# An inverse transform as three passes on high and low parts, in a Hyena and mLSTM encoder layer

## The chip, the cores and the metric

The kernel runs on one core of a Trainium2 chip. The metric is the device time of one execution in microseconds, as the median of several. A core has TensorE (PE in the profile: matrix products into PSUM banks), VectorE (DVE), ScalarE (ACT), GpSimd (POOL) and SyncE (SP), which here only issues DMAs. Each engine runs its own instructions in the order in which they stand in its queue, and waits at an instruction until the others have delivered what it needs.

## The reference

One encoder layer on 2048 rows of 1024 features: a projection, a Hyena group (512 channels) beside an mLSTM group, an output projection, cross-attention to 256 memory rows, and a feed-forward part. What the change touches is the Hyena group's long convolution, made twice (order 0 and order 1) with a filter as long as the sequence, in the frequency domain with zero padding to 4096:

```python
def _hyena(hy, spec, skip):
    L = hy.shape[1]
    u = hy.astype(jnp.float32)
    z, g1, g2 = u[..., :D_HYENA], u[..., D_HYENA:2 * D_HYENA], u[..., 2 * D_HYENA:]
    for o, gate in enumerate((g1, g2)):
        conv = jnp.fft.irfft(jnp.fft.rfft(z, n=2 * L, axis=1) * spec[:, o], n=2 * L, axis=1)[:, :L]
        z = gate * (conv + z * skip[o].astype(jnp.float32))
    return z
```

All data are float32.

## The kernel before, in words

The transform of length 4096 is split into two smaller ones, each done as matrix products on TensorE. In `hyena` (from L789) the first, `spectrum` (L879), multiplies the signal with the matrix `f1` and stores the result in DRAM (`zs0`, `zs1`). The second runs in a loop over 16 blocks (L903), each of two matrices `m`. For each matrix:

- L915 multiplies the loaded signal `t` with the forward matrix `dm[:, m]` into a PSUM bank `pp`; this is a full-precision float32 product, as all those of `hyena` are.
- `response` (L838) has done the same with the filter's block one block ahead; its results are `hr` and `hi`.
- L917 and L918 (ACT) write the bank's two halves, swapped and with a sign, to `xt`; L919 (DVE) multiplies the bank with `hr` into `y`; L920 (POOL) multiplies `xt` with `hi`; L921 (DVE) adds both into `y`. That is the product of two complex spectra.
- `back` (L871) multiplies `y` with the inverse matrix `em[:, m]` (L873) into a bank `pg`; L874 (ACT) copies the bank to `gs`, and after the second matrix L877 (ACT's queue) stores `gs` to DRAM (`zg0`, `zg1`).

`late` (L865) holds `back` of one matrix until the next matrix has been issued, so that the program writes the inverse product one step after its `y`. `load2` (L830) loads, one block ahead, a block's two inverse matrices `em` (128 KB, SP's queue, two buffers) and the signal's block from `zs` (L835). `load_filter` (L821) loads the forward matrices and the filter's block. `xt` and `y` share five buffers (`tb`, tile name `b`); the large tiles (`ta`, name `a`) share ten. After the 16 blocks, a loop over 8 (L926) loads `zg`, multiplies with `e2` and applies the gate; in order 0 that result is the input of order 1.

All this is woven with the input projection (`sweep`, L644, and `natural`, L758): its generator and `hyena`'s are called in turns by the weights that they yield. The projection, like most of the kernel, already computes in three passes. `split` (L341) makes from a float32 tile a high part (`CAST` on ACT, into the type float32r) and a low part (a subtraction on DVE); `mm3` (L336) then issues three matmuls into one bank, high by high, high by low and low by high, on L338, L339 and L340. So these helper lines stand in the profile for every such product, and the tile names tell them apart: `wh`, `wl` are the projection's weights, `xh`, `xl` its input, `mm` its banks, `hy` the banks of `hyena`.

The program's own order is not the order on the engines: a list scheduler, which orders the instructions by a timeline of its own, sets each engine's queue when the kernel is built. A change in one place can thus move instructions near it, on every engine.

Of the kernel before, what the change touches and what calls it, by code (L numbers as in the profile page):

```python
# [9 lines left out]
F32 = mybir.dt.float32  # L10
F32R = mybir.dt.float32r
# [9 lines left out]
CH = 512  # L21
# [111 lines left out]
class Prog:  # L133
# [655 lines left out]
    def hyena(self, es):  # L789
        nc, tc, a = self.nc, self.tc, self.a  # L790
# [7 lines left out]
        def of_block(d, k):  # L798
            return d[4 * k:4 * k + 8].rearrange("(k r) j c -> (r j) k c", k=2)

        sb = es.enter_context(tc.tile_pool(name="h_sb", bufs=1, side="right"))

        def ta():
            return sb.tile([128, 2, CH], F32, tag="a", name="a", bufs=10)

        def tb():
            return sb.tile([128, CH], F32, tag="b", name="b", bufs=5)

        f1 = sb.tile([128, 128], F32, name="f1")
        e2 = sb.tile([128, 64], F32, name="e2")  # L810
        nc.sync.dma_start(out=f1, in_=a["c_f1"])
# [2 lines left out]
        def load1(j2):  # L814
            z = ta()
            js = slice(2 * j2, 2 * j2 + 2)
            for g in range(2):
                nc.sync.dma_start(out=z[own[g]], in_=hy[0, g, :, js])
            return z

        def load_filter(o, i):  # L821
            dm = sb.tile([128, 2, 128], F32, tag="dm", name="dm", bufs=3)
            nc.sync.dma_start(out=dm, in_=a["c_dm"][:, 2 * i:2 * i + 2])
            p, k = divmod(2 * i, 16)
            t = ta()
            for g in range(2):
                nc.sync.dma_start(out=t[own[g]], in_=of_block(fs[o][p, 64 * (p ^ g):64 * (p ^ g) + 64], k))
            return dm, t

        def load2(o, i):  # L830
            em = sb.tile([128, 2, 128], F32, tag="em", name="em", bufs=2)
            nc.sync.dma_start(out=em, in_=a["c_em"][:, 2 * i:2 * i + 2])
            t = ta()
            for g in range(2):
                nc.sync.dma_start(out=t[own[g]], in_=of_block(sds[o][g], 2 * i))  # L835
            return em, t
# [28 lines left out]
        def late(f):  # L865
            if held:
                held.pop()()
            if f is not None:
                held.append(f)

        def back(m, i, em, y, gs, dst):  # L871
            pg = self.hy()
            nc.tensor.matmul(pg, em[:, m], y, start=True, stop=True)  # L873
            nc.scalar.copy(gs[:, m], pg)  # L874
            if m == 1:
                for g in range(2):
                    nc.scalar.dma_start(out=of_block(dst[g], 2 * i), in_=gs[own[g]])  # L877
# [11 lines left out]
        q, fq = [load1(0), load1(1)], []  # L889
# [8 lines left out]
        for o in range(2):  # L898
            gd = gds[o]
            nxt = load2(o, 0)  # L900
            ready = response(0, *fq.pop(0))
            yield 4
            for i in range(16):  # L903
                yield 4.6
                dm, hr, hi = ready
                em, t = nxt
                if i < 14:
                    fq.append(load_filter(o, i + 2))
                if i < 15:
                    nxt = load2(o, i + 1)  # L910
                    ready = response(i + 1, *fq.pop(0))
                gs = ta()
                for m in range(2):
                    pp = self.hy()
                    nc.tensor.matmul(pp, dm[:, m], t[:, m], start=True, stop=True)  # L915
                    xt, y = tb(), tb()
                    nc.scalar.activation(xt[0:64], pp[64:128], AF.Copy, scale=-1.0)  # L917
                    nc.scalar.copy(xt[64:128], pp[0:64])  # L918
                    nc.vector.tensor_tensor(y, pp, hr[:, m], ALU.mult)  # L919
                    nc.gpsimd.tensor_tensor(xt, xt, hi[:, m], ALU.mult)  # L920
                    nc.vector.tensor_tensor(y, y, xt, ALU.add)  # L921
                    late(lambda m=m, i=i, em=em, y=y, gs=gs: back(m, i, em, y, gs, gd))
            late(None)
            nxt = load3(o, 0)
            yield 5
            for j2 in range(8):  # L926
# [14 lines left out]
                y = gate.rearrange("q j (g e) -> q (j g) e", g=8)  # L941
# [542 lines left out]
    def halves(self, src, tags, bufs, eng):  # L1484
        hi, lo = (self.R.tile([128, 512], F32R, tag=n, name=n, bufs=bufs) for n in tags)
        self.nc.scalar.copy(hi, src)  # L1486
        eng.tensor_tensor(lo, src, hi.bitcast(F32), ALU.subtract)  # L1487
        return hi, lo
# [416 lines left out]
```

## Time and profile before

| | us |
|---|---|
| median of 3 timed runs | 3238.39 |
| lowest and highest of them | 3231.79, 3245.16 |
| the profiled execution's own time | 3240.22 |
| its span in the trace | 3238.5 |
| PE busy | 3052.5 |
| DVE busy | 2033.4 |
| ACT busy | 1502.4 |
| POOL busy | 1245.8 |
| mean granted TensorE clock | 0.979 of full |

The span is what the trace shows from the first instruction to the last; the time has a little around it. "Busy" sums the instructions of an engine; matmuls overlap at their ends, so a duration in a PE row is longer than what it adds to PE's stream, which is read from start to start. In the rows, L873 is a line of the kernel, `hy<-b,em` is what it writes and reads, and `x128` a count. A full-precision product is recorded as two matmuls. Where a row says that an instruction waited, the last of its releasers is named.

The inverse products run in two stretches: order 0 from 415 to 602 us and order 1 from 762 to 950 us of the span.

### The profile page before, as it was taken

The page shows a single profiled execution, that of the slowest core. Times are in us where ns is not written, and L with a number is a line of the kernel's source. Part 1 is how long each engine was busy: PE and PEld are TensorE (multiplying, and loading weights), DVE is VectorE, ACT ScalarE, POOL GpSimd, SP SyncE. Part 2 cuts the span into 40 slices and gives each one's busy share as a digit, 9 for nine tenths or more (in the row PEclk, how much of TensorE's full clock was granted, in tenths as well). Part 3 has the DMA queues.
Part 4 walks back from the last instruction along what each step waited for, and adds up shares of the span by engine and source line. Part 5 has one row for each costly group of instructions (what it writes and reads, how often), then busy time and mean ns, then how long its engine had stood idle before and what let it go on. Part 6 is the DMA issues. An engine that isn't in the chain of part 4 may idle for free.

```text
span 3238.5 us, 45244 instructions
## 1 busy us (share of the span) xinstructions
PE 3052.5 (94%) x15241; PEld 2438.0 (75%) x15241; DVE 2033.4 (63%) x3414; ACT 1502.4 (46%) x2873; POOL 1245.8 (38%) x863
## 2 busy tenths in 40 slices
PE   7999899999999876999999998999999999999998
PEld 5655466776668775898988897888788887888876
DVE  7775366447657644776665556656755676566695
ACT  5533366426752423454453445555555543333335
POOL 0122022101213125435251207776855483434483
PEclk9999999999999988999999999999999999999999
DMA  5564768777778598667484537665644475444434
GB/s 187 190 206 162 263 183 221 214 246 199 207 203 262 171 295 261 189 203 230 130 289 131 190 100 233 212 207 165 215 150 153 160 240 160 137 134 149 124 94 166
DMA packets 451634, 617.72 MB, mean 191 GB/s; under 512 B 39615, under 2 KB 247615, under 8 KB 450377
## 3 DMA queue, kind: packets, MB, share of 16 engines
q1 hardware_dynamic: 415268, 556.31, 55.7%
q10 hardware_dynamic: 36132, 58.51, 5.4%
q8 instruction: 121, 1.98, 0.3%
q14 instruction: 113, 0.92, 0.1%
HBM read 416.47 MB, written 198.21 MB: 190 GB/s over the span
## 4 chain that ended last, share of the span: by engine, by line
PE 48%; DMA 9%; DVE 4%; issue 3%; POOL 2%; ACT 2%; SPq 0%; ACTq 0%; DVEq 0%; POOLq 0%
PE mm L340 10%; PE mm L338 10%; PE mm L339 10%; PE hy L340 5%; PE hy L338 5%; PE hy L339 5%; DVE wl L343 1%; DMA wn<-in_xa_wv_dram 1%; DMA va<-vd 1%; DMA wr<-xs 1%; DMA wn<-in_w_out_dram 1%; DMA vw<-o 1%; DMA hg<-hg 1%; ACT wh L343 1%; PE hy L1173 1%
## 5 line engine op out<-in xcount | busy, mean ns | idle before, releaser
L343 DVE TENSOR_TENSOR wl<-wn,wh 128x512 fp32r<-128x512 f32 (+1 forms) x364 | 286.3, 820 | 136.2 <-ACT wh L343 135.7
L1487 DVE TENSOR_TENSOR bl<-wr,bh 128x512 fp32r<-128x512 f32 x213 | 241.7, 1141 | 124.6 <-ACT bh L1486 122.8
L1486 ACT CAST ah<-w 128x512 fp32r<-128x512 f32 x284 | 176.2, 622 | 299.7 <-PE hy L339 154.3
L343 ACT CAST wh<-wn 128x512 fp32r<-128x512 f32 (+1 forms) x364 | 208.7, 617 | 214.6 <-PE mm L339 51.6
L920 POOL TENSOR_TENSOR b<-b,a 128x512 f32<-128x512 f32 x64 | 88.7, 1387 | 519.7 <-ACT b L918 492.4
L338 PE MATMUL mm<-xh,wh 128*128 128x512 f32 x640 | 278.3, 436 | 4.6 <-ACT xh L498 2.3
L339 PE MATMUL mm<-xl,wh 128*128 128x512 f32 x640 | 262.1, 410 | 3.9 <-DVE xl L343 3.4
L1487 DVE TENSOR_TENSOR al<-w,ah 128x512 fp32r<-128x512 f32 x236 | 223.6, 949 | 56.9 <-ACT ah L1486 56.5
L340 PE MATMUL mm<-xh,wl 128*128 128x512 f32 x640 | 256.4, 401 | 0.0
L1486 ACT CAST bh<-wr 128x512 fp32r<-128x512 f32 x232 | 143.6, 620 | 233.8 <-PE mm L340 178.6
L340 PE MATMUL mm<-bh,al 128*128 128x512 f32 x576 | 225.3, 394 | 7.9 <-DVE al L1487 5.1
L338 PE MATMUL mm<-bh,ah 128*128 128x512 f32 x576 | 226.6, 393 | 0.2
L339 PE MATMUL mm<-bl,ah 128*128 128x512 f32 x576 | 225.6, 392 | 0.0
L338 PE MATMUL mm<-act,wh 128*128 128x512 f32 x512 | 200.6, 396 | 1.9 <-ACT wh L343 1.9
L339 PE MATMUL mm<-act,wh 128*128 128x512 f32 x512 | 201.5, 394 | 0.0
L340 PE MATMUL mm<-act,wl 128*128 128x512 f32 x512 | 199.8, 393 | 0.0
L1343 POOL TENSOR_TENSOR ssum<-ssum,sq 128x512 f32<-128x512 f32 x56 | 80.8, 1443 | 277.9 <-ACT sq L1342 274.7
L338 PE MATMUL hy<-bh,ah 128*128 128x512 f32 x448 | 175.2, 391 | 0.0
L339 PE MATMUL hy<-bl,ah 128*128 128x512 f32 x448 | 174.6, 390 | 0.0
L340 PE MATMUL hy<-bh,al 128*128 128x512 f32 x448 | 174.4, 390 | 0.0
L338 PEld LDWEIGHTS mm<-xh,wh 128*128 128x128 f32 x640 | 121.5, 190 | 64.6 <-issue 27.4
L339 PEld LDWEIGHTS mm<-xl,wh 128*128 128x128 f32 x640 | 121.5, 190 | 60.0 <-issue 29.1
(369 smaller groups left out, 8825.8 us busy)
## 6 DMA issues: line engine op xcount, KB each, us to landing
wr<-hc SPq DMA_DIRECT2D x224, 256.0 KB
w<-in_ff_w_dram SPq DMA_DIRECT2D x176, 256.0 KB
hc<-t SPq DMA_DIRECT2D x128, 256.0 KB
wn<-in_w_in_dram SPq DMA_DIRECT2D x100, 256.0 KB
hc<-q SPq DMA_DIRECT2D x96, 256.0 KB
fs<-a SPq DMA_DIRECT2D x32, 512.0 KB
a<-fs SPq DMA_DIRECT2D x64, 256.0 KB
a<-zs SPq DMA_DIRECT2D x64, 256.0 KB
```

What stands on the lines that cost most here:

```text
L338: mm(ps, lh, rh, start=start, stop=False)
L339: mm(ps, lh, rl, start=False, stop=False)
L340: mm(ps, ll, rh, start=False, stop=stop)
L343: both = (self.nc.scalar.copy(hi, src), self.nc.vector.tensor_tensor(lo, src, hi.bitcast(F32), ALU.subtract))
L920: nc.gpsimd.tensor_tensor(xt, xt, hi[:, m], ALU.mult)
L1173: nc.tensor.matmul(dst, nm[:, h], va[:, h], start=True, stop=state is None)
L1343: nc.gpsimd.tensor_tensor(ssum, ssum, sq, ALU.add)
L1486: self.nc.scalar.copy(hi, src)
L1487: eng.tensor_tensor(lo, src, hi.bitcast(F32), ALU.subtract)
```

## The change

The inverse product L873 becomes three passes. `load2` loads the pair of inverse matrices into one raw buffer (`e`, one in place of two) and splits it into high and low parts, two new buffers of each. When `y` is finished, it is split as well: ACT casts it to `vh`, DVE subtracts to get `vl`, again two buffers of each. `back` gets the parts and calls `mm3`. The helpers `split` and `mm3` are as before. The forward products (L842, L915), `f1` and `e2` stay in full precision.

```diff
+        def halves(n):
+            return [sb.tile([128, n], F32R, tag=f"{q}{n}", name=q, bufs=2) for q in ("vh", "vl")]
+
...
         def load2(o, i):
-            em = sb.tile([128, 2, 128], F32, tag="em", name="em", bufs=2)
-            nc.sync.dma_start(out=em, in_=a["c_em"][:, 2 * i:2 * i + 2])
+            e = sb.tile([128, 2, 128], F32, tag="em", name="em", bufs=1)
+            nc.sync.dma_start(out=e, in_=a["c_em"][:, 2 * i:2 * i + 2])
+            em = [t.rearrange("p (m q) -> p m q", m=2) for t in halves(256)]
+            self.split(*em, e)
             t = ta()
...
-        def back(m, i, em, y, gs, dst):
+        def back(m, i, em, vh, vl, gs, dst):
             pg = self.hy()
-            nc.tensor.matmul(pg, em[:, m], y, start=True, stop=True)
+            self.mm3(pg, em[0][:, m], em[1][:, m], vh, vl, True, True)
             nc.scalar.copy(gs[:, m], pg)
...
                     nc.vector.tensor_tensor(y, y, xt, ALU.add)
-                    late(lambda m=m, i=i, em=em, y=y, gs=gs: back(m, i, em, y, gs, gd))
+                    vh, vl = halves(CH)
+                    self.split(vh, vl, y)
+                    late(lambda m=m, i=i, em=em, vh=vh, vl=vl, gs=gs: back(m, i, em, vh, vl, gs, gd))
```

Over the whole program this takes 64 full-precision products from PE and puts 192 passes in their place; ACT gets 64 casts of 512 columns and 32 of 256, and DVE as many subtractions. POOL's order stays the same. On the other engines the scheduler moves instructions in and around both stretches. (In the changed file the lines behind L808 count 3 to 7 higher: L842 is L847, L874 is L879, L915 is L920, L917 and L918 are L922 and L923.)

PE, some blocks into order 0, before. `mm<-xh,wh` and its kin are the projection's passes, `hy<-b,em` an inverse product, `hy<-a,dm` a forward one.

```order
L340 MATMUL mm<-xh,wl 128x512
L873 MATMUL hy<-b,em 128x512 [waits DMAHW3_49,DVE_49]
L915 MATMUL hy<-a,dm 128x512 [waits DMAHW2_49,DMAHW1_49,Activation_49]
L873 MATMUL hy<-b,em 128x512 [waits DVE_49]
L915 MATMUL hy<-a,dm 128x512 [waits Activation_49]
L338 MATMUL mm<-xh,wh 128x512
L339 MATMUL mm<-xl,wh 128x512
L340 MATMUL mm<-xh,wl 128x512
```

PE, some blocks into order 0, in the changed kernel; `hy<-vh`, `hy<-vl,vh` and `hy<-vh,vl` are the three passes of one inverse product.

```order
L340 MATMUL mm<-xh,wl 128x512
L847 MATMUL mm<-a,dm 128x512 [waits DMAHW2_49,DMAHW5_49,DMAHW1_49,Activation_49]
L338 MATMUL hy<-vh 128x512 [waits Activation_49]
L920 MATMUL hy<-a,dm 128x512 [waits DVE_49]
L847 MATMUL mm<-a,dm 128x512 [waits DVE_49,PE_49]
L339 MATMUL hy<-vl,vh 128x512 [waits DVE_49]
L340 MATMUL hy<-vh,vl 128x512
L338 MATMUL mm<-xh,wh 128x512 [waits Activation_49]
```

The one product is now three rows. The first waits for ACT's cast alone and stands ahead of two other products here; the second waits for DVE's subtraction.

ACT, in the middle of a block of order 0, before: `b<-hy` writes `xt`, `a<-hy` copies the inverse product's bank, `zg` is the store, `wh<-wn` a part of the projection's weights, `P` and `cv` belong to the projection.

```order
L917 ACTIVATE b<-hy 64x512 [waits PE_49]
L918 COPY b<-hy 64x512
L343 CAST wh<-wn 128x512 [waits DMAHW4_49]
L874 COPY a<-hy 128x512 [waits PE_49]
L917 ACTIVATE b<-hy 64x512 [waits PE_49]
L918 COPY b<-hy 64x512
L877 DMA zg_2437<-a 64x2x512 [waits DMAHW1_49,Activation_49]
L877 DMA zg_2437<-a 64x2x512 [waits DMAHW2_49]
L706 ACTIVATE cv<-cv 128x1008 [waits DVE_49]
L687 COPY P<-mm 128x512 [waits PE_49]
```

ACT, in the middle of a block of order 0, in the changed kernel; `vh<-b` is the cast of `y`, `vh<-em` that of the matrices.

```order
L922 ACTIVATE b<-hy 64x512 [waits PE_49]
L923 COPY b<-hy 64x512
L343 CAST vh<-b 128x512 [waits DVE_49]
L343 CAST vh<-em 128x256 [waits DMAHW3_49,PE_49]
L879 COPY a<-hy 128x512 [waits PE_49]
L882 DMA zg_2437<-a 64x2x512 [waits Activation_49]
L882 DMA zg_2437<-a 64x2x512 [waits DMAHW4_49]
L687 COPY P<-mm 128x512 [waits PE_49]
L343 CAST vh<-b 128x512 [waits DVE_49]
L701 ACTIVATE cv<-P,par 128x1008 [waits DMAHW0_49,Activation_49]
```

Two new kinds of rows stand ahead of the bank copies L879 and L687: the cast of `y`, which waits for DVE, and the cast of the matrices, which waits for their load and for a product on PE.

SP, one block's loads in order 0, before: `em` are the inverse matrices, `dm` the forward ones, `fs` the filter's block, `zs` the signal's, `wn` and `qt` belong to the projection.

```order
L832 DMA em<-in_c_em_dram 128x256 [waits DMAHW7_49,PE_49]
L823 DMA dm<-in_c_dm_dram 128x256 [waits DMAHW0_49,PE_49]
L372 DMA wn<-in_w_in_dram 128x2x256 [waits DMAHW4_49,DMAHW3_49,DVE_49]
L733 DMA qt<-cv 128x1008 [waits Activation_49]
L827 DMA a<-fs_347 64x2x512 [waits DMAHW5_49]
L827 DMA a<-fs_347 64x2x512 [waits DMAHW6_49]
L835 DMA a<-zs_2435 64x2x512 [waits DMAHW7_49]
```

SP, one block's loads in order 0, in the changed kernel.

```order
L826 DMA dm<-in_c_dm_dram 128x256 [waits DMAHW1_49,PE_49]
L372 DMA wn<-in_w_in_dram 128x2x256 [waits DMAHW4_49,DMAHW2_49,DVE_49]
L835 DMA em<-in_c_em_dram 128x256 [waits DMAHW3_49,DVE_49]
L830 DMA a<-fs_347 64x2x512 [waits DMAHW6_49]
L830 DMA a<-fs_347 64x2x512 [waits DMAHW7_49]
L840 DMA a<-zs_2435 64x2x512 [waits DMAHW0_49]
```

The load of the inverse matrices has moved behind that of the forward ones, and it waits for DVE (the subtraction that frees the raw buffer) where it waited for PE.

## The prediction

> **What bounds the kernel now.** I read the page first for the share of each engine.
>
> ```profile
> span 3238.5 us, 45244 instructions
> ...
> PE 3052.5 (94%) x15241; PEld 2438.0 (75%) x15241; DVE 2033.4 (63%) x3414; ACT 1502.4 (46%) x2873; POOL 1245.8 (38%) x863
> ```
>
> TensorE is busy for 94% of the span; no other engine comes near. That is a mean over stages, so I then read the busy times in windows over the stretch in which the inverse products run. The columns are the window, its length, then busy time and count of PE, PEld, DVE, ACT and POOL, the granted TensorE clock, the DMA share and GB/s.
>
> ```profile
> core 0: us, PE busy (x) PEld busy (x) DVE busy (x) ACT busy (x) POOL busy (x), PEclk, DMA share, GB/s
> ...
> 400.00:520.00 120.00, 117.91 (x421) 77.77 (x420) 80.02 (x117) 82.36 (x133) 26.91 (x19) 1.00 0.71 193
> 520.00:640.00 120.00, 114.37 (x590) 85.35 (x590) 61.78 (x98) 62.49 (x108) 19.03 (x13) 0.97 0.78 224
> 640.00:760.00 120.00, 116.34 (x664) 84.24 (x662) 59.45 (x89) 44.33 (x77) 2.56 (x2) 0.97 0.73 223
> 760.00:880.00 120.00, 117.17 (x426) 77.11 (x425) 80.12 (x118) 81.21 (x135) 25.39 (x19) 1.00 0.72 202
> 880.00:960.00 80.00, 78.42 (x314) 54.49 (x314) 50.22 (x73) 51.52 (x83) 14.82 (x11) 1.00 0.68 189
> ```
>
> PE is idle for 2.1 + 5.6 + 3.7 + 2.8 + 1.6 = 15.8 of these 560 us, while ACT and DVE are busy for some two thirds of the windows where the spectra are multiplied (82.36 and 80.02 of 120). So in this stage the end is set by TensorE's own stream: PE time saved here moves everything behind it forward, and work added to ACT and DVE costs only where PE comes to wait for it.
>
> A busy PE is not the same as PE time used, because matmuls overlap, so I take costs from start to start in PE's timeline (start, duration, what).
>
> ```profile
> 467.33 1.02 PE L873 MATMUL hy<-b,em 128*128 128x512 f32 x2
> 468.19 1.02 PE L915 MATMUL hy<-a,dm 128*128 128x512 f32 x2
> 469.05 1.02 PE L873 MATMUL hy<-b,em 128*128 128x512 f32 x2
> 469.90 1.02 PE L915 MATMUL hy<-a,dm 128*128 128x512 f32 x2
> ...
> 470.99 0.39 PE L339 MATMUL mm<-xl,wh 128*128 128x512 f32 x1
> ...
> 477.15 0.39 PE L339 MATMUL mm<-xl,wh 128*128 128x512 f32 x1
> ```
>
> A full-precision product, which the trace records as two matmuls, takes (469.90 − 467.33) / 3 = 0.857 us from start to start. The two L339 rows are the first and last of an unbroken run of three-pass products, 27 matmuls apart: 6.16 / 27 = 0.228 us for one pass, 0.684 for three.
>
> **The change part by part.**
>
> *Three passes for one product (removed and added on PE).*
>
> ```profile
> L873 PE MATMUL hy<-b,em x128: 590/592/697, 415.0 to 949.6; 128*128 128x512 f32 x128
> ...
>   DVE b L921: 2.1, 2
> ```
>
> These 128 records are 64 products, two in each of 16 blocks, for both orders. Each gives 0.857 − 0.684 = 0.173 us, together 64 × 0.173 = 11.0 us, on the engine that sets the end. The price of three passes is taken from the same lines 338 to 340 at the same shape, so it is well known; −11.0 is the firm term. The Trainium skill, in "FP8 and Floating Point Precision", section "TensorE Precision Notes", says that a true FP32 product makes four passes. By that rule the saving would be one pass for each product, 64 × 0.228 = 14.6 us, and the sum below −10.4 in place of −6.8; the trace differs, since its product takes 0.857 / 0.228 = 3.8 passes, and the sum goes by the trace.
>
> *The parts (added on ACT and DVE).* The casts and subtractions have neighbours of the same form in the weights' parts, and a 128x256 ACT copy is near the cast of the matrices.
>
> ```profile
> L343 ACT CAST wh<-wn x20: 612/620/652, 409.8 to 582.6; 128x512 fp32r<-128x512 f32 x16, 128x544 fp32r<-128x544 f32 x4
> ```
>
> ```profile
> L343 DVE TENSOR_TENSOR wl<-wn,wh x59: 677/685/1102, 410.9 to 956.4; 128x512 fp32r<-128x512 f32 x51, 128x544 fp32r<-128x544 f32 x8
> ```
>
> ```profile
> L779 ACT COPY st<-mm 128x256 f32<-128x256 f32 x19 | 7.1, 372 | 39.0 <-PE mm L340 19.0 <-DMA vd<-st 6.2 <-DMA wn<-in_w_in_dram 4.8
> ```
>
> A block gets on ACT 2 × 0.620 + 0.372 = 1.6 us, on DVE 2 × 0.685 and one subtraction of 256 columns. Nothing in this stage shows that last one; it lies between half the 512-column row and all of it, 0.34 to 0.69, and I take 0.5, the middle, since these rows hold a fixed part too: 1.9 us. How long is a block? SP loads one pair of inverse matrices for each:
>
> ```profile
> 433.79 0.36 SPq L832 DMA_DIRECT2D em<-in_c_em_dram  x1
> ...
> 470.10 0.33 SPq L832 DMA_DIRECT2D em<-in_c_em_dram  x1
> ```
>
> These are four issues, three blocks: 36.31 / 3 = 12.1 us. Of that ACT is busy 82.36 / 120 × 12.1 = 8.3 us and DVE 80.02 / 120 × 12.1 = 8.1. After the change they stand at 9.9 and 10.0, each with some 2.2 us of a block left. So the added 32 × (1.6 + 1.9) = 112 us lie beside PE's stream, at a price of nothing, as long as that cover of 2.2 us a block holds.
>
> *The longer way to each product (a wait on PE).* Behind y now come the cast and the subtraction, 0.620 + 0.685 = 1.3 us, before the last two passes can start. How early is y today?
>
> ```profile
> L921 DVE TENSOR_TENSOR b<-b x64: 670/691/1769, 409.7 to 944.2; 128x512 f32<-128x512 f32 x64
> ```
>
> I set the end of each L921 in the timeline beside the start of its L873, from the first pair (409.7 and 415.0) to the last (944.2 and 949.6), 64 pairs. y is done 3.0 to 8.0 us ahead in 56 of them, 1.8 ahead in one, 0.1 or less in seven; the median is 4.7. So 57 products have room for the 1.3 us, even though the queues are fuller. The seven would each wait 1.3 more if the order stayed, 9.2 us in all. But the order was made anew with the parts in it, and it sets the first pass, which needs only the cast, ahead of the other two, with other matmuls between in 52 of 64 cases. The nearest row is what the present order leaves PE waiting for y, 2.1 us (above). With two engines in the way in place of one I take twice that, +4.2, between 0 and 9.2.
>
> *The matrices' parts and the queues.* One raw buffer in place of two, and its release moves from PE to DVE. SP now loads the next pair when the subtraction is done, not when the product of the block before last has run:
>
> ```profile
> SPq L832 <- PE hy L873: 85.7, 23, 7.8
> ```
>
> 85.7 us of standing on SP go, with the spectra's loads queued behind. What PE waits for from those loads bounds the gain:
>
> ```profile
>   DMA a<-zs: 3.5, 2
> ```
>
> ```profile
>   DMA a<-fs: 5.0, 2
> ```
>
> That is 0 to 8.5 us. I take 0: the wait has not gone, it has moved. The cast of the matrices' high part now waits on ACT, for the load and for the product that frees its buffer, and the filter's matrices still stand on SP behind a wait for PE. On ACT the cast mostly (20 of 32 times) stands right ahead of a copy that itself waits for an inverse product, so it adds little there. The early release of y's buffer (five are shared by xt and y) can only help and is taken at 0.
>
> *The ends of the loops.* After each order's last product come the copy, the store and the load for the next stage. The last pair has room (above), so 0; without that room it is 1.3 for each order, 2.6 in all.
>
> Sum: −11.0 + 4.2 + 0 + 0 + 0 = −6.8 us. The profiled execution took 3240.2, 1.7 us around its span of 3238.5, and would take 3233.4. The median of the three timed runs, 3238.4, lies 1.8 below it; on it I set 3231.6.
>
> **The rivals.**
>
> *No change.* The wait for the parts gives the 11.0 back: 0.17 us for each product, or eight of the 64 waiting the full 1.3. For it: seven stand at the edge already, and both engines lose near half of their slack. Against: the first pass needs only the cast, and the median room is 4.7. Time 3238.4.
>
> *Slower: ACT stands for y.* ACT takes its instructions in order, and the cast of y waits for POOL's product and DVE's sum. Behind it in ACT's row stand the copies that empty the banks which PE waits for (L687, and the copy of the inverse product). Today nothing on ACT waits for y.
>
> ```profile
> L920 POOL TENSOR_TENSOR b<-b,a x64: 1267/1292/2714, 405.3 to 942.8; 128x512 f32<-128x512 f32 x64
> ```
>
> If each cast of y comes right behind xt, ACT stands 1.29 + 0.69 = 2.0 us for it, 4.0 a block. 2.2 are left, so PE loses 1.8 in each of 32 blocks, 57 us, less 11: +46, 3284. It decides from ACT standing over 2.2 us a block; a loss of 0.5% (16 us) needs (16 + 11) / 32 = 0.8 more, 3.0 a block, three quarters of the worst case. For it: L921's longest of 1769 ns against its median of 691, and POOL's 2714 against 1292, show that DVE and POOL can hold each other up, and 96 more subtractions of that kind meet POOL's 64 products. The Trainium skill, "SBUF — State Buffer", section "Who interferes with whom", has a rule for this, that a VectorE instruction with two SBUF inputs contends with a GpSimd instruction that reads SBUF; the trace agrees in those two longest times. Against: in the new order one to a dozen other instructions stand between xt and that cast, and those fill most of the 2.0 us.
>
> *More than the sum.* The loads come early, the 8.5 us go, and no new wait comes: −11.0 − 8.5 = −19.5, 3218.9. For it: SP's 85.7 us. Against: two short waits for zs hold 3.5 of it, and the order of SP's row changed too.
>
> That the change does not do what it says is hardly open: three passes of this shape run in the same stretch at a price that the trace shows.
>
> **How the numbers follow.** The forecast, −2 to −15, has 0.60; no change 0.18; slower 0.10; more than the sum 0.12. 0.5%, 16 us, is about what a measurement of this kernel can tell from no change (its three runs lie 13.4 apart). The forecast and no change lie within it, but for 0.05 of the forecast whose end, with a part of the loads' gain, reaches over. Faster by over 0.5%: 0.12 + 0.05 = 0.17. Slower: 0.10 less 0.01 for a mild case, 0.09. Same: 0.74. The range goes down to 3218, which takes in the best sum, and up to 3247: there PE loses (8.6 + 11.0) / 32 = 0.6 us a block, the mild part of the slower case. Outside lie the rest of the slower case and the trace's noise, under 2 in 10.
>
> **What would show it.** In the changed profile the triples on hy should start 0.23 us apart when unbroken; the weights' wait L338 to L340 on the parts should sum to about 4 us; ACT and DVE should be busy some 99 of the 120 us between 400 and 520; SP's wait ahead of the em load should be gone, or name DVE and be short; the last inverse product should start some 5 to 10 us earlier than 949. I am wrong if PE's idle time between 400 and 960 is over 27 us (15.8 + 11), or if ACT stands for y over 2 us a block, or if PE's idle time falls below 10 us.

## The result, and the profile after

| | us |
|---|---|
| changed kernel, median of 4 runs | 3262.03 (3259.89 to 3263.27) |
| before, median of 4 runs beside it | 3240.47 (3231.79 to 3245.16) |
| ratio, 95% interval | 1.0069, 1.0046 to 1.0092 |
| span of the profiled execution, before and after | 3238.5, 3261.5 |

The change makes the kernel 0.7% slower, by some 22 us. The forecast was 3231.6, within 3218 to 3247, so both the value and the sign of the difference were wrong.

First the page of the changed kernel, span and busy times:

```profile
span 3261.5 us, 45538 instructions
...
PE 3059.2 (94%) x15305; PEld 2460.3 (75%) x15305; DVE 2088.0 (64%) x3510; ACT 1543.8 (47%) x2969; POOL 1247.6 (38%) x863
```

PE's share is the same 94% and says nothing of the loss. The windows of the stretch with the inverse products do (columns as in the prediction: window, length, busy time and count of PE, PEld, DVE, ACT and POOL, granted clock, DMA share, GB/s):

```profile
400.00:520.00 120.00, 113.00 (x416) 78.79 (x414) 91.12 (x134) 86.41 (x148) 26.82 (x18) 0.97 0.69 184
520.00:640.00 120.00, 109.09 (x547) 85.28 (x548) 80.63 (x128) 76.78 (x138) 22.03 (x14) 0.94 0.71 205
640.00:760.00 120.00, 117.12 (x712) 85.33 (x712) 53.64 (x80) 39.48 (x72) 0.00 (x0) 1.00 0.77 243
760.00:880.00 120.00, 111.90 (x429) 78.27 (x428) 91.92 (x139) 86.28 (x150) 24.69 (x18) 0.99 0.73 192
880.00:960.00 80.00, 73.27 (x274) 50.98 (x273) 60.37 (x93) 60.81 (x104) 15.45 (x12) 0.98 0.64 185
```

PE is idle for 7.0 + 10.9 + 2.9 + 8.1 + 6.7 = 35.6 us, where it was 15.8 before. The prediction had named 27 as the bound beyond which it would be wrong. In the stretch between the loops, 640 to 760, nothing is lost (2.9 against 3.7): the loss lies in the two loops over the 16 blocks. Their length is read from the weight loads of the forward product, one group for each order, from the first to the last start. Before:

```profile
L915 PEld LDWEIGHTS hy<-a,dm x64: 186/190/192, 401.3 to 594.5; 128*128 128x128 f32 x64
```

```profile
L915 PEld LDWEIGHTS hy<-a,dm x64: 186/189/192, 752.4 to 939.1; 128*128 128x128 f32 x64
```

The changed kernel:

```profile
L920 PEld LDWEIGHTS hy<-a,dm x64: 186/189/337, 403.9 to 608.3; 128*128 128x128 f32 x64
```

```profile
L920 PEld LDWEIGHTS hy<-a,dm x64: 186/188/192, 763.8 to 962.1; 128*128 128x128 f32 x64
```

The loop of order 0 grew from 193.2 to 204.4 us, that of order 1 from 186.7 to 198.3: 11.2 + 11.6 = 22.8 us, against 23.0 between the spans. Each loop now holds 5.5 us less of product time (half of the 11.0), and takes 11 us more. Windows over the two loops, the first two before, the last two in the changed kernel:

```profile
401.30:594.50 193.20, 186.28 (x685) 123.76 (x684) 131.11 (x192) 133.35 (x218) 43.35 (x30) 0.98 0.72 199
752.40:939.10 186.70, 182.81 (x662) 120.69 (x661) 125.84 (x185) 127.07 (x209) 40.17 (x30) 1.00 0.71 198
...
403.90:608.30 204.40, 187.19 (x715) 132.77 (x716) 160.08 (x237) 151.39 (x260) 46.27 (x30) 0.95 0.67 187
763.80:962.10 198.30, 184.27 (x700) 128.71 (x701) 149.53 (x230) 147.02 (x254) 40.40 (x31) 0.98 0.68 186
```

PE is idle for 10.8 us of the loops before and for 31.2 after: 20.4 of the 22.8. It is also busy for 2.4 us longer, in spite of the shorter products, at a granted clock of 0.95 and 0.98 where it was 0.98 and 1.00.

What does PE wait for there? These are rows of its waits between 400 and 990 us (waiting tile and line, releaser, us in total, times, longest). Before, the copy of the filter's bank by DVE (L846) has one row:

```profile
PE mm L721 <- DVE a L846: 0.4, 1, 0.4
```

In the changed kernel the same copy is L851:

```profile
PE mm L338 <- DVE a L851: 10.0, 6, 4.4
...
PE mm L721 <- DVE a L851: 2.6, 1, 2.6
PE hy L339 <- DVE vl L343: 2.5, 1, 2.5
...
PE hy L338 <- ACT vh L343: 1.5, 4, 0.5
...
PE mm L727 <- DVE a L851: 1.2, 1, 1.2
...
PE mm L847 <- DVE a L851: 1.1, 1, 1.1
```

All rows of the view sum to 20.5 us before (15 rows) and to 39.4 after (20 rows). For the parts themselves, where the prediction had looked, PE waits 2.5 + 1.5 = 4.0 us. For L851 it waits 10.0 + 2.6 + 1.2 + 1.1 = 14.9: of the 18.9 more, 14.5 are these. Most are waits of the projection's products (`mm`), which have no data from the changed product at all.

One place shows how that comes about. `response` writes the filter's product into one of the four `mm` banks, the same that the projection uses, and ACT (L848, L849) and DVE (L850, L851) copy it out. Here is PE in the changed kernel, some rows between 502 and 522 us:

```profile
502.47 1.02 PE L847 MATMUL mm<-a,dm 128*128 128x512 f32 x2
...
504.61 1.10 PE L847 MATMUL mm<-a,dm 128*128 128x512 f32 x2 [1.11 <-ACT cv L706]
```

```profile
516.68 1.96 PE L847 MATMUL mm<-a,dm 128*128 128x512 f32 x4
521.18 0.47 PE L338 MATMUL mm<-xh,wh 128*128 128x512 f32 x1 [2.54 <-DVE a L851]
```

And DVE at the same place:

```profile
515.66 0.69 DVE L924 TENSOR_TENSOR b<-hy,a 128x512 f32<-128x512 f32 x1 [3.77 <-ACT b L923]
...
517.95 0.69 DVE L924 TENSOR_TENSOR b<-hy,a 128x512 f32<-128x512 f32 x1 [0.18 <-ACT b L923]
518.56 1.04 DVE L343 TENSOR_TENSOR vl<-em,vh 128x256 fp32r<-128x256 f32 x1
519.64 0.69 DVE L850 COPY a<-mm 64x512 f32<-64x512 f32 x1
520.34 0.69 DVE L851 COPY a<-mm 64x512 f32<-64x512 f32 x1
```

And the last of ACT's copies of the same bank:

```profile
518.84 0.58 ACT L849 COPY a<-mm 64x512 f32<-64x512 f32 x1
```

The products of one block's response were made at 502.47 and 504.61 (two records each). The first of their banks is not emptied until 521.03, since DVE's copies stand in its row behind two spectra's products (L924) of the block in progress and a subtraction of the matrices; and DVE itself stood for 3.77 us ahead of 515.66, for ACT's copy of a forward product (L923). ACT's copies come late as well, the last at 518.84; DVE's end last. At 516.68 PE makes the next block's two response products. Now all four `mm` banks hold responses, no pass of the projection can start, and PE stands from 518.64 until 521.18, 0.15 us after L851's end. Before, the same pair of products and its copies at a like place were this:

```profile
499.65 1.88 PE L842 MATMUL mm<-a,dm 128*128 128x512 f32 x4
...
510.32 1.88 PE L842 MATMUL mm<-a,dm 128*128 128x512 f32 x4
```

```profile
506.40 0.69 DVE L846 COPY a<-mm 64x512 f32<-64x512 f32 x1
...
508.44 0.69 DVE L846 COPY a<-mm 64x512 f32<-64x512 f32 x1
```

Both banks are empty at 509.13, before the next pair at 510.32. I set the end of each response product beside the end of its L846 or L851, 64 pairs for each kernel: the median is 6.4 us before and 10.6 after. For ACT's last copy (L844, L849) it is 4.8 and 8.9, so the whole response is emptied later, by both engines, and DVE's copy is the last of the four for all 64. The time to DVE's copy, "time to empty", is used below for every kernel; it is an evaluation of the same rows, not a view of its own.

Standing costs PE more than the stand itself, since the granted clock falls behind it. Two places in the changed kernel, in windows, and the longest stand, which lies at the second of them:

```profile
502.97:506.38 3.41, 1.62 (x4) 0.30 (x2) 3.32 (x6) 3.35 (x6) 0.52 (x1) 1.00 0.80 267
506.38:509.79 3.41, 3.40 (x8) 2.72 (x9) 3.38 (x7) 1.27 (x3) 1.25 (x1) 0.50 0.49 108
...
591.72:595.13 3.41, 1.86 (x9) 0.91 (x7) 3.41 (x7) 3.33 (x6) 2.69 (x2) 1.00 0.47 129
...
598.54:605.37 6.83, 6.00 (x25) 5.93 (x26) 3.83 (x7) 3.15 (x6) 0.00 (x0) 0.50 0.61 189
```

```profile
599.37 0.56 PE L338 MATMUL mm<-wh,xh 128*128 128x272 f32 x1 [4.39 <-DVE a L851]
```

At the first place PE stood for 1.11 us (ahead of 504.61, above) and for 0.69, and then had a clock of 0.50 for 3.41 us, in which passes of 512 columns start 0.43 us apart, where they start 0.23 apart at full clock: about half of that time is lost. At the second the clock is at 0.50 from 595.13, the beginning of the stand of 4.39 us (594.98 to 599.37), to 605.37, so that about half of the 6.00 us in which PE is busy behind the stand, 3 us, is lost on top of it. Around the stand of 2.54 us that ends at 521.18 the clock stayed at 1.00. The Trainium skill, "TensorE: Matmul & The Clock Gate", section "Part 1: The HAM clock gate", says that the clock falls to half after an idle window of about 3.4 us; these rows do not agree with it, since PE was busy for 1.62 and 1.86 of the 3.41 us ahead of the two falls. In the nine falls of both kernels between 400 and 990 us PE had been busy for 22 to 55% of the 3.41 us ahead (worked out from the same traces).

### The profile page after: what moved, and what is told of

Read it like the earlier page. It is cut to its first block, busy times and chain, and to the rows that moved or that the text cites. A ratio compares the mean times of both kernels' runs of the same rounds, so it can differ in the third digit from the quotient of the medians.

```text
span 3261.5 us, 45538 instructions
## 1 busy us (share of the span) xinstructions
PE 3059.2 (94%) x15305; PEld 2460.3 (75%) x15305; DVE 2088.0 (64%) x3510; ACT 1543.8 (47%) x2969; POOL 1247.6 (38%) x863
## 4 chain that ended last, share of the span: by engine, by line
PE 55%; DMA 8%; DVE 5%; issue 3%; ACT 2%; POOL 2%; SPq 0%; ACTq 0%; DVEq 0%; POOLq 0%
PE mm L338 12%; PE mm L340 12%; PE mm L339 12%; PE hy L338 5%; PE hy L340 5%; PE hy L339 5%; DVE bl L1494 1%; DMA rw<-rows 1%; DVE wl L343 1%; DMA wr<-xs 1%; DMA wn<-in_xa_wo_dram 1%; PE hy L1180 1%; ACT wh L343 1%; PE hy L1182 1%; DMA wn<-in_w_out_dram 1%
## 5 line engine op out<-in xcount | busy, mean ns | idle before, releaser
L321 POOL TENSOR_TENSOR b<-b 128x512 f32<-128x512 f32 x32 | 59.1, 1847 | 274.2 <-PE mm L721 120.3
```

The source lines that it names most:

```text
L321: nc.gpsimd.tensor_tensor(e[1], f, b, ALU.subtract)
```

## The experiments

The letters in the expectations are the theories of the time: A, the parts load ACT and DVE; B, the three passes cost more than the product; C, any new order of the queues gives or takes as much; D and E, the parts have too few buffers; F, the first pass, set early, holds its bank; G, the way of a matrix from forward product to copied result (13.5 us before, 17.3 after, medians) is longer, and the program keeps only so many matrices under way; H, the large buffers are held longer. What the section above shows of the response's banks became my theory (R) only when all runs were in. "x" is the ratio to the kernel before, timed beside each. The last two columns are of the one profiled execution, whose own time can lie off the median (by 14 us in e5, 13 in e9); in e13 and e17 the sum of waits holds one of 4.6 and 4.5 us that lies ahead of the window but for its end.

| kernel | median us | x, 95% interval | PE waits 400 to 990 | time to empty, median |
|---|---|---|---|---|
| before | 3240.47 | 1 | 20.5 | 6.4 |
| changed | 3262.03 | 1.0069, 1.0046 to 1.0092 | 39.4 | 10.6 |
| e1_passes_only | 3224.03 | 0.9966, 0.9951 to 0.9981 | 21.5 | 4.9 |
| e2_parts_unused | 3239.70 | 1.0014, 1.0001 to 1.0028 | 24.5 | 6.2 |
| e3_act_only | 3242.60 | 1.0015, 0.9999 to 1.0030 | 22.0 | 5.5 |
| e4_dve_only | 3234.51 | 0.9995, 0.9982 to 1.0008 | 18.8 | 6.5 |
| e5_y3 | 3252.25 | 1.0052, 1.0025 to 1.0079 | 35.2 | 10.6 |
| e6_em3 | 3255.22 | 1.0052, 1.0034 to 1.0070 | 37.1 | 9.9 |
| e7_y_parts | 3257.72 | 1.0059, 1.0039 to 1.0078 | 35.8 | 10.1 |
| e8_em_parts | 3223.22 | 0.9951, 0.9936 to 0.9966 | 18.6 | 5.8 |
| e9_low_first | 3280.31 | 1.0139, 1.0114 to 1.0165 | 55.0 | 14.5 |
| e10_early_hold | 3236.26 | 0.9992, 0.9981 to 1.0002 | 16.8 | 4.5 |
| e11_low_first_pool | 3287.49 | 1.0156, 1.0142 to 1.0170 | 55.6 | 14.2 |
| e12_null | 3239.78 | 1.0004, 0.9993 to 1.0016 | 22.5 | 6.4 |
| e13_late2 | 3232.61 | 0.9974, 0.9962 to 0.9987 | 20.7 | 4.9 |
| e14_filler | 3282.95 | 1.0135, 1.0121 to 1.0149 | 40.3 | 11.1 |
| e15_dve_cast | 3256.44 | 1.0056, 1.0042 to 1.0069 | 33.6 | 9.6 |
| e16_a11 | 3263.41 | 1.0068, 1.0055 to 1.0081 | 36.7 | 10.6 |
| e17_both3 | 3248.94 | 1.0035, 1.0021 to 1.0048 | 36.2 | 9.7 |
| e18_before_late2 | 3217.94 | 0.9942, 0.9927 to 0.9957 | 11.5 | 3.8 |

### Which part of the change costs

**e1_passes_only** issues the three passes but makes no low parts: `y` is rounded by its own addition and stands for both parts, and the matrices are cast once.

```diff
-                    vh, vl = halves(CH)
-                    self.split(vh, vl, y)
+                    vh = vl = y
...
-            self.split(*em, e)
+            nc.scalar.copy(em[0], e)
```

> The inverse product runs as three passes, but y is written rounded and used as both of its parts, and the matrices are only cast once (a cast of 256 columns on ACT in each block), so the output lacks the low parts. No work on DVE is added. Theory A (the parts' work on ACT and DVE delays the copies that free the banks, and PE waits for banks): the saving of the passes shows nearly whole, 3240 - 11 = 3229, with PE's lost time in both stretches as before. Rival B (the passes themselves are the cost: a bank held longer, or the second pass waiting): still 3250 or more. Rival C (the new order by itself, whatever work it holds): anything between 3225 and 3265.

Measured 0.9966: 11 us faster, as the prediction's −11.0 for the passes. B falls.

**e2_parts_unused** makes all parts as the changed kernel does and then multiplies in full precision with the raw tiles (the raw matrices have two buffers, as before the change).

```diff
-            self.mm3(pg, em[0][:, m], em[1][:, m], vh, vl, True, True)
+            nc.tensor.matmul(pg, em[:, m], y, start=True, stop=True)
```

> All parts are made as in the changed kernel, but the inverse product stays one full-precision product of the raw tiles; the parts are read by nobody. Theory A: the loss without the saving, 3262 + 11 = 3273. Rival B: no loss, 3240. Rival C: anything between 3230 and 3265.

**e3_act_only** is e2 with the casts alone, **e4_dve_only** with subtractions alone (a tile minus itself); nothing reads them.

```diff
-                    self.split(vh, vl, y)
+                    nc.scalar.copy(vh, y)                               # e3
+                    nc.vector.tensor_tensor(vh, y, y, ALU.subtract)     # e4
```

> Only ACT's share of the parts is made (the casts of y and of the matrices), read by nobody; the product is the full-precision one. Theory A with DVE as the engine that matters (the banks that PE waits for are freed by a DVE copy): 3240 to 3248. Theory A with ACT as that engine (the cast of y stands in ACT's row for POOL and DVE): 3258 to 3273. Rival B: 3240.

> Only DVE's share is made: a subtraction of 512 columns behind each y and one of 256 for each pair of matrices, with no cast (the tile minus itself), read by nobody; the product is the full-precision one. Theory A with DVE as the engine that matters: 3258 to 3273. With ACT: 3240 to 3248. Rival B: 3240.

Measured 1.0014, 1.0015 and 0.9995. In e2 both engines do all the added work, in the window 400 to 520:

```profile
400.00:520.00 120.00, 120.00 (x431) 79.22 (x429) 95.54 (x143) 95.30 (x161) 26.90 (x19) 1.00 0.68 195
```

DVE and ACT are busy for 95 of 120 us, more than in the changed kernel (91 and 86), and PE is never idle. So the work of the parts is nearly free, as the prediction had it, and A falls; what costs is that the product waits for it.

**e7_y_parts** splits only `y` (the matrices are cast and stand for both parts), **e8_em_parts** only the matrices (`y` rounded).

```diff
-            self.split(*em, e)            # e7
+            nc.scalar.copy(em[0], e)
...
-                    self.split(vh, vl, y)      # e8
+                    vh = vl = y
```

> Three passes with y in two parts, as in the changed kernel, but the matrices are only cast: their high part stands for both, so the output lacks their low part, and DVE makes no subtraction for them. Theory D: still 3250 to 3262, since y's buffers are as before. Theory E: about half the loss or less, since the matrices' high part is still held until the product.

> Three passes with the matrices in two parts, as in the changed kernel, but y is written rounded and used as both of its parts, so the output lacks y's low part; y stays in its five buffers. Theory D: 3225 to 3232, since nothing of y waits for two buffers. Theory E: 3250 to 3262.

Measured 1.0059 and 0.9951. e1 and e8 differ in the matrices' low parts alone, and so do e7 and the changed kernel; within each pair the intervals overlap, so the matrices' parts cost nothing that shows. e1 and e7 differ in `y`'s parts alone (0.9%), and so do e8 and the changed kernel (1.2%); between e7 and e8 lie 1.1%, some 35 us. So `y`'s parts, on the way to the product, take all of it. PE's waits for L851 go with them: these are e7's rows, and then e8's.

```profile
PE mm L741 <- DVE a L851: 5.2, 2, 2.7
PE mm L847 <- DVE a L851: 3.5, 4, 1.8
PE mm L721 <- DVE a L851: 2.6, 1, 2.6
```

```profile
PE mm L721 <- DVE a L851: 1.0, 2, 0.6
PE mm L338 <- DVE a L851: 0.3, 1, 0.3
```

**e12_null** gives the kernel before a third buffer for the matrices, so that the order is made anew and nothing else changes.

```diff
-            em = sb.tile([128, 2, 128], F32, tag="em", name="em", bufs=2)
+            em = sb.tile([128, 2, 128], F32, tag="em", name="em", bufs=3)
```

> The kernel before with three buffers in place of two for the inverse matrices, and nothing else: SP's wait for a buffer goes and the scheduler makes a new order, but the work is the same. C (orders differ by chance by tens of us): off by 10 or more either way. F and G: within 5 of 3238; a gain of up to 8 if the loads that stood behind SP's wait mattered.

Measured 1.0004: this new order of the same work costs nothing, and C has no support from it.

### Buffers, and the order of the passes

**e5_y3** gives `y`'s parts three buffers, **e6_em3** the matrices' parts, **e17_both3** both, and **e16_a11** the large tiles eleven.

```diff
-            return [sb.tile([128, n], F32R, tag=f"{q}{n}", name=q, bufs=2) for q in ("vh", "vl")]
+            return [sb.tile([128, n], F32R, tag=f"{q}{n}", name=q, bufs=3) for q in ("vh", "vl")]   # e17
...
-            return sb.tile([128, 2, CH], F32, tag="a", name="a", bufs=10)
+            return sb.tile([128, 2, CH], F32, tag="a", name="a", bufs=11)    # e16
```

> The changed kernel with three buffers in place of two for each part of y. Theory A fell with the first four runs (making the parts unused costs 4, not 33). Theory D: the parts are held until the product, so with two buffers the cast of y can run only two matrices ahead of the products, and the whole chain of a matrix goes in step with PE. If y's buffers are what limits it: 3225 to 3235. If the matrices' buffers are (E): 3262 as the changed kernel. If it is the new order by chance (C): anything between 3225 and 3265.

> The changed kernel with three buffers in place of two for each part of the matrices; y's parts keep two. Theory D (y's buffers): 3262 as the changed kernel. Theory E (the cast of the next matrices waits on ACT for the last product that reads the buffer, and holds ACT's row): 3225 to 3235. C: anything between.

> The changed kernel with eleven large buffers in place of ten. Theory H (loads and response copies wait for large buffers, which the later products hold longer): 3235 to 3250. G: 3258 to 3264, no change.

> The changed kernel with three buffers for all four kinds of parts (y's and the matrices', high and low) in place of two, and nothing else: the inverse product is held back by one matrix as before. It is the kernel of e13_late2 without the second matrix held back. Theory G (the chain of a matrix got longer by the parts, and the program keeps only so many matrices under way, so the loop is paced by the chain): buffers alone do not put more matrices under way; the chain stays at 16 to 18 us, the loop of order 0 at 6.4 to 6.8 us a matrix, and the time at 3250 to 3262 with a kernel before of 3240, a ratio of 1.003 to 1.007. Rival J (the gain of e13 came from the buffers, because y's and the matrices' parts have to be deep together): as e13, 3230 to 3240, a ratio of 0.996 to 1.000, pace at or below 6.2 us a matrix.

Measured 1.0052, 1.0052, 1.0068 and 1.0035. H falls, and so do D and E, which had expected 3225 to 3235 of e5 and of e6. One more buffer of either kind moves the time within the interval of the changed kernel; both together may take back half of the loss (its interval just meets the changed kernel's). The time to empty stays near 10 in all four.

**e9_low_first** issues the pass with `y`'s low part first, so that the three passes stand together and nothing starts before the subtraction; **e11_low_first_pool** also moves that subtraction to POOL.

```diff
-            self.mm3(pg, em[0][:, m], em[1][:, m], vh, vl, True, True)
+            nc.tensor.matmul(pg, em[0][:, m], vl, start=True, stop=False)
+            nc.tensor.matmul(pg, em[0][:, m], vh, start=False, stop=False)
+            nc.tensor.matmul(pg, em[1][:, m], vh, start=False, stop=True)
...
-                    self.split(vh, vl, y)
+                    nc.scalar.copy(vh, y)                                               # e11
+                    nc.gpsimd.tensor_tensor(vl, y, vh.bitcast(F32), ALU.subtract)
```

> The changed kernel with the three passes in another order: high by low goes first, so that no pass is ready before both parts are, and the three stand together on PE. All the work, the buffers and the path to the last pass stay the same. Theory F (the first pass needs only the cast, is set ahead, and takes one of the four hy banks until the last pass and the copy are done, so the forward products and through them ACT and the response's copies come later): 3225 to 3232. Theory G (the 1.3 us longer path through ACT and DVE to each product): still 3250 to 3262. C (a new order by chance): anything between 3225 and 3265.

> As e9, with the subtraction for y's low part on POOL in place of DVE. If DVE's share of the work still costs something once the passes stand together, this is 3 to 8 faster than e9; if not, it is the same within 5, or slower, since POOL takes about 1.3 for it in place of 0.7 and its product for the next matrix stands behind.

**e10_early_hold** is e8 with a matmul of 64 columns that takes the product's bank early.

```diff
+            nc.tensor.matmul(pg[:, 0:64], em[0][:, m], em[0][:, m, 0:64], start=True, stop=True)
             self.mm3(pg, em[0][:, m], em[1][:, m], vh, vl, True, True)
```

> The kernel of e8 (three passes, matrices in parts, y rounded and used as both parts; 3223), with one more matmul of 64 columns ahead of each product, which reads only the matrices and writes into the product's bank; the passes then overwrite it, so it adds about 64 x 0.03 = 2 us of PE and nothing else but that it takes the bank early (20 to 40 matmuls ahead in a third of the cases). Theory F: the loss comes back without y's parts, 3245 to 3265. Theory G: 3225.

Measured 1.0139, 1.0156 and 0.9992. F falls: taking the early pass away made it worse, and the early hold cost e8's gain, 13 us with 64 more matmuls, not the 35. Those 13 us do not lie in the loops, which last 359.6 us in e10's trace and 365.7 in e8's; where they come from is open. e9 lies above what G and C had allowed as well, and e11 within e9's interval. These two slowest kernels have the longest time to empty, 14.5 and 14.2 us.

### How far the product is held back

**e13_late2** is the changed kernel with the inverse product held back by two matrices in place of one, and three buffers for all parts.

```diff
-        def late(f):
-            if held:
-                held.pop()()
+        def late(f, n=1):
+            while len(held) >= (n if f is not None else 1):
+                held.pop(0)()
...
-                    late(lambda m=m, i=i, em=em, vh=vh, vl=vl, gs=gs: back(m, i, em, vh, vl, gs, gd))
+                    late(lambda m=m, i=i, em=em, vh=vh, vl=vl, gs=gs: back(m, i, em, vh, vl, gs, gd), 2)
```

> The changed kernel with the inverse product held back by two matrices in the program in place of one, and three buffers for every part so that it can be. Theory G (a matrix's chain from the forward product to the copy is 17.3 us long in the changed kernel and 13.5 before, and the program keeps only so many matrices under way, so the loop is paced by the chain): 3225 to 3245. Theory H (the ten large buffers are what keeps the matrices under way few): 3255 to 3265, no change. C (order by chance): anything.

Measured 0.9974: faster than the kernel before, with the same three passes. PE no longer waits for L851 at all, and the window 400 to 520 is full:

```profile
400.00:520.00 120.00, 119.83 (x455) 84.74 (x456) 97.29 (x143) 93.85 (x160) 26.78 (x19) 0.99 0.74 196
```

With e17 beside it the gain over the changed kernel splits: the buffers may give 0.3%, holding back two another 0.6%.

**e18_before_late2** does the same to the kernel before, whose inverse products are in full precision.

```diff
-                    late(lambda m=m, i=i, em=em, y=y, gs=gs: back(m, i, em, y, gs, gd))
+                    late(lambda m=m, i=i, em=em, y=y, gs=gs: back(m, i, em, y, gs, gd), 2)
```

> The kernel before (full-precision inverse products, no parts) with the inverse product held back by two matrices in place of one, and three buffers for the matrices in place of two. Theory G: its chain of 13.5 us is short enough for the 2.2 matrices under way, so holding back one more gains little: 3233 to 3242, a ratio of 0.998 to 1.001, and the gain of e13 (0.9974) is the three passes' own. Rival K (holding back by two helps any such loop, and the gain of e13 is of the order and not of the passes): as e13 or better, 3225 to 3233, a ratio of 0.995 to 0.998.

Measured 0.9942, 3217.94 us: the fastest kernel of the study, and a miss for G, which expected no gain. Holding back helps without the three passes too, and more than with them: by the two ratios, from two sets of runs, the passes still cost 0.9974 / 0.9942, some 0.3%. In PE's waits of e18 nearly nothing is left of the response's copy:

```profile
PE mm L338 <- DVE a L846: 0.2, 1, 0.2
```

One of its response pairs and its last copy:

```profile
496.51 1.88 PE L842 MATMUL mm<-a,dm 128*128 128x512 f32 x4
```

```profile
501.31 0.69 DVE L846 COPY a<-mm 64x512 f32<-64x512 f32 x1
```

Both banks are free 3.6 us after the second product, where the pair of before that was shown took 7.6 (509.13 less 501.53).

**e14_filler** is the changed kernel with more of the projection woven into the loops (the weight of a block from 4.6 to 5.6), **e15_dve_cast** casts `y` on DVE.

```diff
-                yield 4.6
+                yield 5.6        # e14
...
-                    self.split(vh, vl, y)
+                    nc.vector.tensor_copy(vh, y)                                        # e15
+                    nc.vector.tensor_tensor(vl, y, vh.bitcast(F32), ALU.subtract)
```

> The changed kernel with more of the projection woven into the two loops over the blocks (the weight of a block is 5.6 in place of 4.6, the total weight 311 in place of 279), so the loops hold about 9% more of the projection's work and the other stretches as much less. Theory G: PE has more to do while a chain runs; 5 to 20 of the loss come back, 3242 to 3257. Theory A's rest (ACT and DVE too full in the loops): worse, 3265 or more, since the projection brings its own copies.

> The changed kernel with y's cast on DVE in place of ACT, so that add, cast and subtraction stand on one engine and two hand-overs between queues go; DVE gets 64 x 0.7 = 45 us more, ACT 40 less. Theory G, by hand-overs: y to low part takes 1.5 to 2 in place of 3.3, and about half of the loss comes back, 3240 to 3252. Theory A's rest (DVE's load): 3265 or more.

Measured 1.0135 and 1.0056, both outside what G had expected. In e14 work meant to fill PE's gaps made it slower, and why is open: its waits between 400 and 990 us sum to 40.3, hardly more than the changed kernel's 39.4, with 6.8 for L851; ahead of the first block PE stands 8.1 us for the filter's load, where the changed kernel stands 0.7. e15 is no test of G, since the way did not get shorter: the low part is ready 2.8 us after `y` (median), 3.0 in the changed kernel, not the 1.5 to 2 expected. PE waits only 1.7 us for L851 there, but 12.5 us for the parts that DVE now makes; the sum of waits falls only from 39.4 to 33.6.

## Why the prediction was wrong

*Three passes for one product, −11.0: right.* e1 and e8 have it (−0.34 and −0.49%). In the changed kernel three passes in a row start 0.23 us apart, as forecast:

```profile
528.08 0.39 PE L338 MATMUL hy<-vh 128*128 128x512 f32 x1
...
528.53 0.39 PE L340 MATMUL hy<-vh,vl 128*128 128x512 f32 x1
```

*The parts, at nothing: right as a load.* Their durations are those taken from the neighbours, with 0.41 and 0.42 for the matrices where I had 0.37 and 0.5:

```profile
L343 ACT CAST vh<-b x64: 602/621/639, 414.1 to 966.9; 128x512 fp32r<-128x512 f32 x64
L343 DVE TENSOR_TENSOR vl<-b,vh x64: 668/683/1286, 414.7 to 967.6; 128x512 fp32r<-128x512 f32 x64
...
L343 ACT CAST vh<-em x30: 389/406/410, 422.0 to 953.0; 128x256 fp32r<-128x256 f32 x30
L343 DVE TENSOR_TENSOR vl<-em,vh x30: 408/422/1065, 422.5 to 954.8; 128x256 fp32r<-128x256 f32 x30
```

ACT and DVE are busy for 86 and 91 of the 120 us between 400 and 520, where the text expected some 99, since the blocks take longer there; in e2 it is 95. e2, which does all of the work unread, costs at most 0.28%.

*The longer way to each product, +4.2 between 0 and 9.2: this step failed.* It asked how much of the 4.7 us between `y` and its product was left, and priced the wait at the product, which measured 4.0 us. That 4.2 comes so near is luck: the 2.1 us that it doubles are no wait of PE. In the kernel before, between 400 and 990 us, that row is one of the weight loads (PEld), and PE itself stood at L873 once, for 1.0 us:

```profile
PEld hy L873 <- DVE b L921: 2.1, 2, 1.3
```

The step that failed is what it left out. Those 4.7 us were not a reserve, they come from the order. In the changed kernel the last pass again stands 4.4 us (median) behind its parts, so the product moved with its data; and the parts are ready not 1.3 but some 3 us after `y` (1.6 to the end of the cast, 1.3 to that of the subtraction), since each stands in a queue. What is queued around the longer way was not followed: on DVE and ACT, the copies that empty the response's banks. Its price was 14.5 of the 18.9 us of added waits, most of them on products that have nothing to do with the inverse product, with a lower clock in the same loops. By e7 against e8 the step is worth some 35 us, not 4.

*The matrices' parts and the queues, 0: right.* SP's 85.7 us have become a wait for DVE, as the text allowed, though not a short one, and e8 gains what the passes give, a little more at most:

```profile
SPq L835 <- DVE vl L343: 57.6, 26, 5.5
```

The 5.0 us for `fs` in its bound were one wait counted on two engines, 2.9 on the weight loads and 2.1 on PE, ahead of the first block.

*The ends of the loops, 0* played no part that the rows show: the loops' own growth of 22.8 us holds the whole difference, and the last pass of the last inverse product starts at 972.8, 23 us later than the product of before (949.6), where 5 to 10 us earlier was expected.

*The rival "ACT stands for y"* had the right kind of cause, a copy that empties a bank and stands behind work on `y`, at the wrong place and with the wrong point of decision. ACT's row of waits, 400 to 980 us:

```profile
ACT vh L343 <- DVE b L926: 21.3, 14, 2.9
```

That is 0.7 us a block, under the 2.2 from which the rival was to decide and far under the 3.0 for a loss of 0.5%. And e13 is faster with more of it (31.8 us). A mean cover for each block could not show that the four banks of `mm` are all taken for a few microseconds in some blocks.

**What is shown and what is not.** Shown: the cost comes with the parts of `y` that a product waits for (e2, e7, e8), not from the passes, the engines' load or the buffers alone; and it goes when the product is held back by one more matrix (e13, with the buffers of e17, which alone take back half at most). The medians of the time to empty part the kernels without exception: 3.8 to 6.5 us in those within 0.15% of before or faster, 9.6 to 14.5 in those slower by 0.35% or more. Those of ACT's last copy part them as well, 2.1 to 4.8 against 6.3 to 12.4. That the banks are the cause is read from the rows, and at one place in full; no run changed only the banks or only the place of their copies. With more buffers (e5, e6, e17) the waits for L851 fall by half and others come, so that the banks are the largest place of the loss in the changed kernel and not all of it. G as it was stated falls with e18, which gained where it expected nothing; and the way from forward product to copy is 19.4 us in e13 and 16.9 in e18 (medians), two kernels faster than before: a longer way did not set the pace by itself. Open are where e14 loses its time, why the scheduler sets those copies later when `y`'s way is longer, and what remains of the passes' cost, 0.3%, when two matrices are held back.

## What to carry to other kernels

Room between an operand and its use, read in a trace, was no slack here: the order had set it, and the longer way to the operand moved the use and copies queued near it. For each instruction added to such a way, list what stands behind it on its engine, and above all the copies that empty shared banks, and count the banks that are held at once. When a product gets a longer way, hold it back by one more step first; here that alone, on the kernel before, gave more (0.9942) than the passes with it (0.9974).

## What the hardware showed that was not expected

The subtraction of 256 columns took 0.42 us in the median but up to 1.065, and 1.04 in the row shown at 518.56, while POOL multiplied (its row started at 518.05 and took 1.27). Of the 32 subtractions 13 met a product of POOL, with a median of 0.81 us; the 19 others took 0.43 at most. PE's clock fell to 0.50 behind 3.41 us in which PE was busy for about half the time and no stand was over 1.2 us, and stayed at 1.00 around a stand of 2.54, so that several short stands together could cost what a single longer one did not.
